# A decoder trunk on one core: order of the loads, roots and slab copies in its first stage

## The chip, the cores and the metric

The kernel runs on one core of one Trainium2 chip. The metric is the device time of one execution in microseconds. Three runs were timed, and one more execution was recorded by the hardware profiler; all readings of the trace below come from that one. The engines are named as the profile names them: PE does the matmuls (PEld loads its weights), DVE is the vector engine, ACT the scalar engine, POOL is GpSimd, and SP issues most of the DMAs.

## What is computed

One layer of a decoder over 512 positions of width 1024: a norm, one wide input projection, three groups of heads side by side (a gated delta rule, a sparse attention, a causal pooling), an output projection with a residual, a second norm and an MLP with a squared ReLU. Only the part at the start matters for this change.

```python
def rms_norm(x, g):
    xf = x.astype(jnp.float32)
    return (xf * lax.rsqrt(jnp.mean(xf * xf, axis=-1, keepdims=True) + EPS) * g).astype(x.dtype)

h = rms_norm(x, norm_mix[l])          # x: 512 x 1024
proj = h @ w_in[l]                    # w_in: 1024 x 2974, split among the heads
```

Everything is in float32.

## The kernel before

**Tiles.** The 512 positions are four tiles of 128 (`NT`), the width of 1024 is eight pieces of 128 (`KC`). A float32 product is made of three matmuls in a rounded type: each operand is split into a high part, its rounded copy, and a low part, the rest; high by high, high by low and low by high are summed.

**The first stage** (lines 153 to 330) brings x through the norm, transposes it, splits it, and multiplies it with the first slab of the projection's weights: 286 columns, loaded in two halves of 512 rows, here called slabs 0 and 1 (`dma_a`, L206). Each tile `i` goes through these steps:

- `load_x(i)` (L200): one DMA of 512 KB.
- `norm_sq(i)` (L153): the squares and their sum, on ACT (`sq`, `ss`).
- `norm_root(i)` (L159): the inverse square root of the sum. It starts from a guess made out of the bits of the number, by a shift (L164) and a multiply with add (L165) on DVE, and goes through three Newton steps of two instructions (L168 and L169 on POOL for tiles 1 to 3, L171 and L172 on DVE for tile 0).
- `norm_b(i)` (L175): x by the root and by the norm's weights `gm_b`, in two halves on DVE (`scr`, L179); then eight transposes on PE (L183).
- `norm_c(i)` (L186): the high part is copied out of PSUM by ACT (`hTh`, L191), the low part is made by DVE (`hTl`, L192).

A slab `q` is copied to its high part by ACT (`hi_a`, L210) and its low part is made by DVE (`lo_a`, L215 and L218, one instruction of 128x1144). `proj_a(i, k0, k1)` (L245) multiplies pieces `k0` to `k1` of tile `i` with them, three matmuls for each piece: 24 for a whole tile. A row of matmuls on a tile of ones (L235) stands ahead of it all.

**What sets the order.** Instructions of the first stage are recorded with `kp`, which keeps them on each engine in the order in which the program writes them; the calls from `norm_sq(0)` to `proj_a(3, 0, 8)` (L302 to L326) are that order. Each engine takes its instructions strictly in order and waits at one whose inputs aren't there. Instructions behind the first stage are placed by a scheduler, from its own estimate of when each could run; a change at the start can so move rows far behind it. The DMAs go through SP in the order written.

**What follows.** The other columns of the projection come in slabs of 256 columns (cast on ACT at L134, low part on DVE at L135, matmuls at L143 to L145), at first between the last matmuls of `proj_a`. Behind it stand the heads, up to about 385 us, and the MLP. `rsqrt` (L101), used by the heads, and `x2_norm` (L1239), used ahead of the MLP, make their first guess in the same two instructions.

Of the kernel before, what the change touches and what calls it, by code (L numbers as in the profile page):

```python
# [20 lines left out]
P = 128  # L21
# [16 lines left out]
def trunk_kernel(ctx, tc, x, norm_mix, w_in, conv_w, a_log, dt_bias, gdn_norm, nsa_q_norm, nsa_k_norm,  # L38
# [62 lines left out]
    def rsqrt(y, a, n, p=P):  # L101

        V.tensor_single_scalar(y.bitcast(I32), a.bitcast(I32), 1, ALU.logical_shift_right)
        V.tensor_scalar(y.bitcast(I32), y.bitcast(I32), -1.0, float(0x5EF759DF - 0x80000000), ALU.mult, ALU.add)
        t = sml.tile([P, n], F32, tag=f"rs{n}", name=nm("rs"))[:p]
        for _ in range(3):
            if n == 1:
                V.scalar_tensor_tensor(t, y, a, y, ALU.mult, ALU.mult)
            else:
                V.tensor_tensor(t, y, y, ALU.mult)  # L110
                V.tensor_tensor(t, t, a, ALU.mult)
            V.scalar_tensor_tensor(y, t, -1.5, y, ALU.add, ALU.mult)
# [46 lines left out]
    def norm_root(i):  # L159
# [3 lines left out]
        kp(V.tensor_scalar(ss, ss, 0.5 / D, 0.5 * EPS, ALU.mult, ALU.add))  # L163
        kp(V.tensor_single_scalar(r.bitcast(I32), ss.bitcast(I32), 1, ALU.logical_shift_right))  # L164
        kp(V.tensor_scalar(r.bitcast(I32), r.bitcast(I32), -1.0, float(0x5EF759DF - 0x80000000), ALU.mult, ALU.add))  # L165
        for _ in range(3):
# [43 lines left out]
    def hi_a(q):  # L210
        rs, hi, lo = ra[q]
        for r, k in rs:
            kp(S.copy(hi[:, k], r))

    def lo_a(q):  # L215
        rs, hi, lo = ra[q]
        for r, k in rs:
            kp(V.tensor_tensor(lo[:, k], r, f32v(hi[:, k]), ALU.subtract))  # L218
        for k in range(4):
            for c, t_ in enumerate((hi, lo)):  # L220
                slab_a[c].append(t_[:, k])

# [5 lines left out]
    S.activation(one1, one1, AF.Square)  # L228
    load_x(0)
    gm_b = bc(norm_mix[0], "gm_b", D)  # L230
    gmix = [gm_b[:, ts(b, T)] for b in range(2)]

    wps = pn()
    for _ in range(22):
        kp(PE.matmul(wps[:, 0:P], onep, onep, start=True, stop=True))  # L235
    for i in range(2):
        ra.append(dma_a(i))
        load_x(i + 1)
    load_x(3)

# [3 lines left out]

    def proj_a(i, k0, k1):  # L245

        if k0 == 0:
            aps[i] = pm()
        ps = aps[i][:, :286]
        for k in range(k0, k1):  # L250
            ah, al = hTh[:, k, ts(i, P)], hTl[:, k, ts(i, P)]
            kp(PE.matmul(ps, ah, slab_a[0][k], start=k == 0, stop=False))
            kp(PE.matmul(ps, ah, slab_a[1][k], start=False, stop=False))
            kp(PE.matmul(ps, al, slab_a[0][k], start=False, stop=k == KC - 1))

# [47 lines left out]
    norm_root(0)  # L303
    hi_a(0)
    norm_sq(1)
    norm_b(0)
    norm_root(1)
    lo_a(0)
    norm_c(0)
    hi_a(1)  # L310
    lo_a(1)
    norm_sq(2)
    norm_sq(3)
    proj_a(0, 0, 8)
    norm_b(1)
    norm_root(2)
    norm_c(1)
    proj_a(1, 0, 4)
    norm_root(3)
    norm_b(2)  # L320
    edge = norm_c(2)
    proj_a(1, 4, 8)
    edge += norm_b(3),
    proj_a(2, 0, 8)
    norm_c(3)
    proj_a(3, 0, 8)  # L326
    consts, first = ExitStack(), ExitStack()
# [911 lines left out]
    def x2_norm(i):  # L1239
# [4 lines left out]
        V.tensor_scalar(ss, ss, 0.5 / D, 0.5 * EPS, ALU.mult, ALU.add)  # L1244
        V.tensor_single_scalar(r.bitcast(I32), ss.bitcast(I32), 1, ALU.logical_shift_right)
        V.tensor_scalar(r.bitcast(I32), r.bitcast(I32), -1.0, float(0x5EF759DF - 0x80000000), ALU.mult, ALU.add)
        for _ in range(3):
# [169 lines left out]
```

## Time and profile before

| what | us |
|---|---|
| three runs | 724.2, 726.22, 729.62 |
| their median | 726.22 |
| the profiled execution | 724.06 |
| its span, from the first to the last instruction | 722.3 |
| PE busy in the span | 696.5 (96%) |
| DVE busy | 556.1 (77%) |
| ACT busy | 385.1 (53%) |
| POOL busy | 172.6 (24%) |

The busy share is an average over stages. To see what a change at the start can be worth, the stretches have to be looked at one by one, and in the first of them what each engine waits for. A row of the timeline is: start in us, length in us, engine, line and operation, what is written and read, how many; in brackets how long the engine sat idle before it, and what ended that. A row `x2` counts two instructions that follow each other. The chain of waits is followed back from the last instruction of the span: at each step to what released it, or to the instruction before it on its engine.

### The profile page before, as it was taken

What the parts mean: (1) busy time and instruction counts of PE and PEld (TensorE: products, weight loads), DVE (VectorE), ACT (ScalarE), POOL (GpSimd) and SP (SyncE); (2) the same over time, 40 slices, a digit from 0 to 9 for tenths busy, and PEclk for the clock granted to TensorE, in tenths of its full rate; (3) what the DMA queues carried; (4) which work ended last, traced back from release to release, by engine and by line L of the source; (5) the groups of instructions that cost most, each with busy time, mean ns of one, the idle gap of its engine ahead of it and who ended that gap; (6) DMA issues with size and microseconds to landing.
All of it is one profiled execution on the core that took longest, in us unless ns stands there. A gap on an engine that the chain in (4) does not pass through costs nothing.

```text
span 722.3 us, 13313 instructions
## 1 busy us (share of the span) xinstructions
PE 696.5 (96%) x5155; PEld 572.3 (79%) x5155; DVE 556.1 (77%) x1061; ACT 385.1 (53%) x768; POOL 172.6 (24%) x257
## 2 busy tenths in 40 slices
PE   8999999999999998999899999999999999999997
PEld 7888887888988776776679878888888888878885
DVE  5688998878686788887554997977958686796846
ACT  5455835565754558677543945444444444544430
POOL 5730004222123310000030330505032140504223
PEclk9999999999999999999999999999999999999999
DMA  7343223132410602221120153324041333302103
GB/s 224 91 107 103 72 60 89 32 96 60 131 31 4 234 1 59 88 88 31 59 87 2 59 176 119 114 89 144 18 158 59 120 113 113 121 23 95 58 1 116
DMA packets 49922, 62.20 MB, mean 86 GB/s; under 512 B 5494, under 2 KB 42564, under 8 KB 49860
## 3 DMA queue, kind: packets, MB, share of 16 engines
q1 hardware_dynamic: 48996, 61.16, 27.1%
q8 instruction: 40, 0.66, 0.4%
q10 hardware_dynamic: 864, 0.20, 0.1%
q14 instruction: 22, 0.18, 0.1%
HBM read 59.25 MB, written 2.10 MB: 85 GB/s over the span
## 4 chain that ended last, share of the span: by engine, by line
PE 71%; DVE 17%; DMA 4%; ACT 4%; issue 3%; POOL 1%; SPq 1%; DVEq 0%; ACTq 0%; POOLq 0%
PE ps L143 17%; PE ps L145 17%; PE ps L144 17%; PE ps L424 5%; PE ps L1139 2%; PE ps L799 2%; DMA w2r<-in_w_ffn_dram 2%; DVE bl L1293 2%; PE ps L1125 1%; DVE lw L135 1%; PE ps L587 1%; DMA x<-in_x_dram 1%; PE ps L1100 1%; ACT P L1106 1%; DVE x L1386 1%
## 5 line engine op out<-in xcount | busy, mean ns | idle before, releaser
L144 PE MATMUL ps<-h2l,hw 128*128 128x512 f32 (+1 forms) x280 | 105.1, 376 | 0.1
L145 PE MATMUL ps<-h2h,lw 128*128 128x512 f32 (+1 forms) x280 | 104.9, 376 | 0.0
L143 PE MATMUL ps<-h2h,hw 128*128 128x512 f32 (+1 forms) x280 | 103.8, 374 | 0.0
L1300 POOL TENSOR_TENSOR al<-gF,ah 128x512 fp32r<-128x512 f32 x24 | 38.1, 1586 | 220.5 <-ACT ah L1299 181.0
L143 PE MATMUL ps<-bh,ah 128*128 128x512 f32 x224 | 88.5, 395 | 1.2 <-DVE x L1386 1.2
L144 PE MATMUL ps<-bl,ah 128*128 128x512 f32 x224 | 88.2, 394 | 0.0
L145 PE MATMUL ps<-bh,al 128*128 128x512 f32 x224 | 84.6, 394 | 0.0
L1386 DVE TENSOR_TENSOR x<-ps,x 128x512 f32<-128x512 f32 x112 | 72.7, 680 | 6.0 <-PE ps L145 5.8
L1293 DVE TENSOR_TENSOR bl<-w2r,bh 128x1024 fp32r<-128x1024 f32 x40 | 57.8, 1447 | 6.1 <-ACT bh L1292 6.1
L144 PEld LDWEIGHTS ps<-h2l,hw 128*128 128x128 f32 x280 | 52.7, 188 | 10.6 <-DVE h2l L1264 0.3
L143 PEld LDWEIGHTS ps<-h2h,hw 128*128 128x128 f32 x280 | 52.3, 188 | 10.2
L145 PEld LDWEIGHTS ps<-h2h,lw 128*128 128x128 f32 x280 | 52.6, 188 | 9.7
L1300 POOL TENSOR_TENSOR al<-gS,ah 128x512 fp32r<-128x512 f32 x32 | 53.4, 1687 | 24.8 <-ACT ah L1299 23.5
L1292 ACT CAST bh<-w2r 128x1024 fp32r<-128x1024 f32 x40 | 41.8, 1047 | 24.1 <-PE ps L145 23.5
L135 DVE TENSOR_TENSOR lo<-raw,hi 128x512 fp32r<-128x512 f32 (+1 forms) x76 | 42.3, 580 | 14.4 <-ACT hi L134 11.9
L134 ACT CAST hi<-raw 128x512 fp32r<-128x512 f32 (+1 forms) x76 | 37.0, 518 | 28.5 <-DMA raw<-in_w_in_dram 10.4
L143 PEld LDWEIGHTS ps<-bh,ah 128*128 128x128 f32 x224 | 42.1, 188 | 12.1 <-ACT ah L1299 0.9
L145 PEld LDWEIGHTS ps<-bh,al 128*128 128x128 f32 x224 | 42.1, 188 | 9.7
L144 PEld LDWEIGHTS ps<-bl,ah 128*128 128x128 f32 x224 | 42.2, 188 | 9.5
L1299 ACT CAST ah<-gS 128x512 fp32r<-128x512 f32 x32 | 19.7, 620 | 50.9 <-DVE gS L1368 24.5
L134 ACT CAST hw<-raw 128x1024 fp32r<-128x1024 f32 x32 | 32.1, 1046 | 24.6 <-PE ps L144 22.2
L135 DVE TENSOR_TENSOR lw<-raw,hw 128x1024 fp32r<-128x1024 f32 x32 | 40.1, 1287 | 6.2 <-ACT hw L134 6.2
(373 smaller groups left out, 1701.9 us busy)
## 6 DMA issues: line engine op xcount, KB each, us to landing
raw<-in_w_ffn_dram SPq DMA_DIRECT2D x32, 512.0 KB, 3.8
w2r<-in_w_ffn_dram SPq DMA_DIRECT2D x32, 512.0 KB, 5.5
raw<-in_w_in_dram SPq DMA_DIRECT2D x24, 256.0 KB, 3.0
raw<-in_w_in_dram SPq DMA_DIRECT2D x36, 128.0 KB, 2.6
x<-in_x_dram SPq DMA_DIRECT2D x8, 512.0 KB, 6.7
raw<-in_cmp_w_dram SPq DMA_DIRECT2D x32, 128.0 KB, 2.7
raw<-in_w_out_dram SPq DMA_DIRECT2D x8, 512.0 KB, 4.1
out_dram<-x SPq DMA_DIRECT2D x8, 256.0 KB, 2.0
```

What stands on the lines that cost most here:

```text
L134: {"A": S.copy, "V": V.tensor_copy, "G": G.tensor_copy}[e[0]](hi[:, k], r)
L135: {"V": V, "G": G}[e[1]].tensor_tensor(lo[:, k], r, f32v(hi[:, k]), ALU.subtract)
L143: PE.matmul(ps, ah, bh, start=start, stop=False, **kw)
L144: PE.matmul(ps, ah, bl, start=False, stop=False, **kw)
L145: PE.matmul(ps, al, bh, start=False, stop=stop, **kw)
L424: PE.matmul(ps[:, ts(i, 256)], a_[:, k, ts(2 * b + i, P)], w_, start=(k == 0 and n_ == 0 and i == 0), stop=(k == KC - 1 and n_ == 2 and i ...
L799: PE.matmul(ps[halves[p], ts(s_, 64)], lhsT(halves[p], s_), rhs(halves[p], s_), start=True, stop=True)
L1292: S.copy(hi, src)
L1293: V.tensor_tensor(lo, src, f32v(hi), ALU.subtract)
L1299: S.copy(hi, src)
L1300: G.tensor_tensor(lo, src, f32v(hi), ALU.subtract)
L1386: V.tensor_tensor(x2[i][:, cs], acc[bk, t_], x2[i][:, cs], ALU.add)
```

## The change

It has five parts, all but the last in the first stage.

- The second tile of x is loaded right behind the first, ahead of `gm_b` and of the slabs.
- The first slab's high part is copied by two engines, two pieces by ACT and two by DVE. Slabs are entered in `slab_a` when they are copied, not when their low part is made.
- The order is written anew: the squares of tile 1 come ahead of the slab's copy; the scaling of tile 1 comes ahead of the low part of slab 1, as do the squares of tile 2; the root of tile 2 comes behind that low part and ahead of `norm_c(1)`. Three more matmuls on ones follow the transposes of tile 0.
- `proj_a` goes through a tile in six parts of four matmuls: three with slab 0 (high by high, high by the slab's low part, low by high), then three with slab 1, of which the last is the one that needs the low part of slab 1. For tile 0 that last part is put behind two parts of tile 1.
- The first guess of a root is one instruction: a multiply by -0.5 and an add on the bits as a number, here and in `rsqrt` and `x2_norm` (21 roots in all).

```diff
     def norm_root(i):
         kp(V.tensor_scalar(ss, ss, 0.5 / D, 0.5 * EPS, ALU.mult, ALU.add))
-        kp(V.tensor_single_scalar(r.bitcast(I32), ss.bitcast(I32), 1, ALU.logical_shift_right))
-        kp(V.tensor_scalar(r.bitcast(I32), r.bitcast(I32), -1.0, float(0x5EF759DF - 0x80000000), ALU.mult, ALU.add))
+        kp(V.tensor_scalar(r.bitcast(I32), ss.bitcast(I32), -0.5, float(0x5EF759DF - 0x80000000), ALU.mult, ALU.add))
...
     def hi_a(q):
         rs, hi, lo = ra[q]
-        for r, k in rs:
-            kp(S.copy(hi[:, k], r))
+        r = rs[0][0]
+        if q == 0:
+            kp(S.copy(hi[:, 0:2], r[:, 0:2]))
+            kp(V.tensor_copy(hi[:, 2:4], r[:, 2:4]))
+        else:
+            kp(S.copy(hi, r))
...
     load_x(0)
+    load_x(1)
     gm_b = bc(norm_mix[0], "gm_b", D)
...
-    for _ in range(22):
-        kp(PE.matmul(wps[:, 0:P], onep, onep, start=True, stop=True))
+    def warm(n):
+        for _ in range(n):
+            kp(PE.matmul(wps[:, 0:P], onep, onep, start=True, stop=True))
+
+    warm(22)
     for i in range(2):
         ra.append(dma_a(i))
-        load_x(i + 1)
-    load_x(3)
+    for i in range(2, NT):
+        load_x(i)
...
-    def proj_a(i, k0, k1):
+    def proj_a(i, n0, n1):
...
+        for n in range(n0, n1):
+            q, a_, w_ = ((0, hTh, 0), (0, hTh, 1), (0, hTl, 0), (4, hTh, 0), (4, hTl, 0), (4, hTh, 1))[n]
+            for k in range(q, q + 4):
+                kp(PE.matmul(ps, a_[:, k, ts(i, P)], slab_a[w_][k], start=(n == 0 and k == 0),
+                             stop=(n == 5 and k == KC - 1)))
...
     norm_sq(0)
     norm_root(0)
-    hi_a(0)
     norm_sq(1)
     norm_b(0)
     norm_root(1)
+    warm(3)
+    hi_a(0)
     lo_a(0)
     norm_c(0)
     hi_a(1)
+    proj_a(0, 0, 5)
+    norm_b(1)
+    norm_sq(2)
     lo_a(1)
-    norm_sq(2)
-    norm_sq(3)
-    proj_a(0, 0, 8)
-    norm_b(1)
     norm_root(2)
     norm_c(1)
-    proj_a(1, 0, 4)
+    norm_sq(3)
+    proj_a(1, 0, 2)
+    proj_a(0, 5, 6)
     norm_root(3)
+    proj_a(1, 2, 6)
     norm_b(2)
     edge = norm_c(2)
-    proj_a(1, 4, 8)
+    proj_a(2, 0, 3)
     edge += norm_b(3),
-    proj_a(2, 0, 8)
+    proj_a(2, 3, 6)
     norm_c(3)
-    proj_a(3, 0, 8)
+    proj_a(3, 0, 6)
```

Three places show what the order of the instructions becomes. The first is SP's queue at the start; before (x_92 is tile 0, x_124 tile 1; raw_121 and raw_128 are slabs 0 and 1, each in two DMAs):

```order
L202 DMA x_92<-in_x_dram 128x1024
L98 DMA gm_b<-in_norm_mix_dram 128x1024
L127 DMA raw_121<-in_w_in_dram 128x4x268
L127 DMA raw_121<-in_w_in_dram 128x4x18
L202 DMA x_124<-in_x_dram 128x1024
L127 DMA raw_128<-in_w_in_dram 128x4x268
L127 DMA raw_128<-in_w_in_dram 128x4x18
```

And now (tile 1 is x_94, slab 0 raw_123):

```order
L200 DMA x_92<-in_x_dram 128x1024
L200 DMA x_94<-in_x_dram 128x1024
L98 DMA gm_b<-in_norm_mix_dram 128x1024
L126 DMA raw_123<-in_w_in_dram 128x4x268
L126 DMA raw_123<-in_w_in_dram 128x4x18
L126 DMA raw_128<-in_w_in_dram 128x4x268
L126 DMA raw_128<-in_w_in_dram 128x4x18
```

Tile 1 went ahead of `gm_b` and of both DMAs of slab 0. The second place is DVE from the second half of tile 0's scaling to the first step of tile 2's root; before (scr_266 and scr_267 are tile 1 scaled, lo_120 and lo_127 the low parts of slabs 0 and 1, ss_235 the sum of tile 2):

```order
L179 SCALAR_TENSOR_TENSOR scr_204<-x_92,r_188,gm_b 128x512
L163 TENSOR_SCALAR ss_200<-ss_200 128x1
L164 TENSOR_SCALAR r_217<-ss_200 128x1
L165 TENSOR_SCALAR r_217<-r_217 128x1
L218 TENSOR_TENSOR lo_120<-raw_121,hi_119 128x1144
L192 TENSOR_TENSOR hTl<-ps_207,hTh 128x4x128
L192 TENSOR_TENSOR hTl<-ps_208,hTh 128x4x128
L218 TENSOR_TENSOR lo_127<-raw_128,hi_126 128x1144
L179 SCALAR_TENSOR_TENSOR scr_266<-x_124,r_217,gm_b 128x512
L179 SCALAR_TENSOR_TENSOR scr_267<-x_124,r_217,gm_b 128x512
L163 TENSOR_SCALAR ss_235<-ss_235 128x1
```

And now (scr_257 and scr_258 are tile 1 scaled, lo_122 and lo_127 the low parts, ss_271 the sum of tile 2):

```order
L177 SCALAR_TENSOR_TENSOR scr_202<-x_92,r_188,gm_b 128x512
L162 TENSOR_SCALAR ss_198<-ss_198 128x1
L163 TENSOR_SCALAR r_215<-ss_198 128x1
L213 CAST hi_121<-raw_123 128x572
L223 TENSOR_TENSOR lo_122<-raw_123,hi_121 128x1144
L190 TENSOR_TENSOR hTl<-ps_205,hTh 128x4x128
L190 TENSOR_TENSOR hTl<-ps_206,hTh 128x4x128
L177 SCALAR_TENSOR_TENSOR scr_257<-x_94,r_215,gm_b 128x512
L177 SCALAR_TENSOR_TENSOR scr_258<-x_94,r_215,gm_b 128x512
L223 TENSOR_TENSOR lo_127<-raw_128,hi_126 128x1144
L162 TENSOR_SCALAR ss_271<-ss_271 128x1
```

One instruction of the guess is gone, half a copy has come in front of slab 0's low part, and the low part of slab 1 went from before the scaling of tile 1 to behind it. The third place is PE from the transposes of tile 2 to those of tile 3; before (ps_323 and ps_324 are the transposes of tile 2, ps_353 and ps_354 those of tile 3, ps_295 the projection of tile 1, ps_363 that of tile 2; the rows left out repeat the three matmuls on ps_295 for the other pieces):

```order
L183 MATMUL ps_323<-ident,scr_319 128x128 x4
L183 MATMUL ps_324<-ident,scr_320 128x128 x4
L252 MATMUL ps_295<-hi_126,hTh 128x286
L253 MATMUL ps_295<-lo_127,hTh 128x286
L254 MATMUL ps_295<-hi_126,hTl 128x286
...
L183 MATMUL ps_353<-ident,scr_349 128x128 x4
L183 MATMUL ps_354<-ident,scr_350 128x128 x4
L252 MATMUL ps_363<-hi_119,hTh 128x286
```

And now (ps_335 and ps_336 are the transposes of tile 2, ps_366 and ps_367 those of tile 3, ps_349 is the projection of tile 2):

```order
L181 MATMUL ps_335<-ident,scr_331 128x128 x4
L181 MATMUL ps_336<-ident,scr_332 128x128 x4
L260 MATMUL ps_349<-hi_121,hTh 128x286 x4
L260 MATMUL ps_349<-lo_122,hTh 128x286 x4
L260 MATMUL ps_349<-hi_121,hTl 128x286 x4
L181 MATMUL ps_366<-ident,scr_362 128x128 x4
L181 MATMUL ps_367<-ident,scr_363 128x128 x4
L260 MATMUL ps_349<-hi_126,hTh 128x286 x4
```

Between the transposes of tiles 2 and 3 stood the second half of tile 1's projection; now it is done before them, and the first half of tile 2's stands there.

More of the change, by code (lines that the diff above doesn't have):

```diff
@@ L101, in rsqrt @@
     def rsqrt(y, a, n, p=P):
-        V.tensor_single_scalar(y.bitcast(I32), a.bitcast(I32), 1, ALU.logical_shift_right)
-        V.tensor_scalar(y.bitcast(I32), y.bitcast(I32), -1.0, float(0x5EF759DF - 0x80000000), ALU.mult, ALU.add)
+        V.tensor_scalar(y.bitcast(I32), a.bitcast(I32), -0.5, float(0x5EF759DF - 0x80000000), ALU.mult, ALU.add)
         t = sml.tile([P, n], F32, tag=f"rs{n}", name=nm("rs"))[:p]
@@ L211, in hi_a @@
         rs, hi, lo = ra[q]
-        for r, k in rs:
-            kp(S.copy(hi[:, k], r))
+        r = rs[0][0]
[4 more added lines that the diff above has]
+            kp(S.copy(hi, r))
+        for k in range(4):
+            for c, t_ in enumerate((hi, lo)):
+                slab_a[c].append(t_[:, k])
     def lo_a(q):
@@ L218, in lo_a @@
             kp(V.tensor_tensor(lo[:, k], r, f32v(hi[:, k]), ALU.subtract))
-        for k in range(4):
-            for c, t_ in enumerate((hi, lo)):
-                slab_a[c].append(t_[:, k])
     xt, xw, ra, nr, nps = {}, {}, [], {}, {}
@@ L243, in trunk_kernel @@
     aps = {}
-    def proj_a(i, k0, k1):
-        if k0 == 0:
+    def proj_a(i, n0, n1):
+        if n0 == 0:
             aps[i] = pm()
         ps = aps[i][:, :286]
[L250 to L254, printed above, removed]
+        for n in range(n0, n1):
[3 more added lines that the diff above has]
+                             stop=(n == 5 and k == KC - 1)))
     def block_mask(name, cond_pattern):
@@ L1244, in x2_norm @@
         V.tensor_scalar(ss, ss, 0.5 / D, 0.5 * EPS, ALU.mult, ALU.add)
-        V.tensor_single_scalar(r.bitcast(I32), ss.bitcast(I32), 1, ALU.logical_shift_right)
-        V.tensor_scalar(r.bitcast(I32), r.bitcast(I32), -1.0, float(0x5EF759DF - 0x80000000), ALU.mult, ALU.add)
+        V.tensor_scalar(r.bitcast(I32), ss.bitcast(I32), -0.5, float(0x5EF759DF - 0x80000000), ALU.mult, ALU.add)
         for _ in range(3):
```

## The prediction

> **What bounds the kernel now.** I read the stages first: the busy times of each engine in four stretches, cut at 25.28 us (the last tile's transposes), 120 us and 385 us. The columns are the length, then busy time and count for PE, PEld, DVE, ACT and POOL, then the granted clock.
>
> ```profile
> core 0: us, PE busy (x) PEld busy (x) DVE busy (x) ACT busy (x) POOL busy (x), PEclk, DMA share, GB/s
> 0.00:25.28 25.28, 20.43 (x116) 18.48 (x117) 14.90 (x37) 12.54 (x25) 16.08 (x65) 0.93 0.57 181
> 25.28:120.00 94.72, 94.69 (x618) 78.28 (x619) 82.44 (x193) 52.70 (x114) 20.27 (x58) 1.00 0.33 88
> 120.00:385.00 265.00, 248.90 (x2928) 203.75 (x2927) 198.82 (x556) 163.00 (x414) 45.14 (x80) 1.00 0.23 70
> 385.00:722.30 337.30, 332.47 (x1498) 271.81 (x1496) 259.95 (x276) 156.87 (x216) 91.14 (x56) 1.00 0.28 91
> ```
>
> From 25.28 to 120 us PE is busy for 94.69 of 94.72 us. Whatever lets PE enter that stretch earlier, or with less left to do, moves all behind it. From 120 to 385 us PE is idle for 265.00 - 248.90 = 16.1 us in many small waits. The change edits the first 25 us. There the chain of waits names the order of events; its columns are start, length and what.
>
> ```profile
> 2.74 6.99 DMA x<-in_x_dram
> 9.81 1.16 ACT sq L156 x2
> 11.45 0.57 DVE lo L218
> ...
> 17.29 0.21 PE ps L252
> 18.16 0.45 PE ps L183 x4
> 18.63 0.59 ACT hTh L191
> 19.25 1.29 DVE hTl L192 x2
> ...
> 24.39 0.76 DVE scr L179
> 25.28 0.64 PE ps L183 x4
> ```
>
> The second tile of x, issued fifth at 2.74 us, lands at 9.73 us; its squares, its root and then those of the next tiles follow each other down to the scaling of the fourth tile at 24.39 us (L179) and its transposes at 25.28 us. Up to there PE is fed by this chain; behind it PE is its own bound. The timeline shows how the chain runs, on DVE, then POOL (the roots of tiles 1 to 3, six small instructions each), then ACT.
>
> ```profile
> 8.09 1.42 DVE L179 SCALAR_TENSOR_TENSOR scr<-x,r,gm_b 128x512 f32<-128x512 f32 x2
> 11.45 1.35 DVE L218 TENSOR_TENSOR lo<-raw,hi 128x1144 fp32r<-128x1144 f32 x1
> 12.72 1.28 DVE L192 TENSOR_TENSOR hTl<-ps,hTh 128x512 fp32r<-128x512 f32 x2
> 13.92 1.34 DVE L218 TENSOR_TENSOR lo<-raw,hi 128x1144 fp32r<-128x1144 f32 x1
> 16.23 1.42 DVE L179 SCALAR_TENSOR_TENSOR scr<-x,r,gm_b 128x512 f32<-128x512 f32 x2 [0.97 <-POOL r L169]
> 17.74 0.15 DVE L164 TENSOR_SCALAR r<-ss 128x1 int32<-128x1 int32 x1
> 17.93 0.15 DVE L165 TENSOR_SCALAR r<-r 128x1 int32<-128x1 int32 x1
> 20.90 1.42 DVE L179 SCALAR_TENSOR_TENSOR scr<-x,r,gm_b 128x512 f32<-128x512 f32 x2
> ```
>
> ```profile
> 11.63 1.39 POOL L168 TENSOR_SCALAR rs<-r,ss 128x1 f32<-128x1 f32 x1 [3.77 <-DVE r L165]
> 13.92 1.47 POOL L169 TENSOR_SCALAR r<-rs,r 128x1 f32<-128x1 f32 x1
> 15.93 0.27 POOL L169 TENSOR_SCALAR r<-rs,r 128x1 f32<-128x1 f32 x1
> 18.18 0.34 POOL L168 TENSOR_SCALAR rs<-r,ss 128x1 f32<-128x1 f32 x1 [1.99 <-DVE r L165]
> 20.24 0.26 POOL L169 TENSOR_SCALAR r<-rs,r 128x1 f32<-128x1 f32 x1
> 21.08 1.29 POOL L168 TENSOR_SCALAR rs<-r,ss 128x1 f32<-128x1 f32 x1 [0.58 <-DVE r L165]
> ```
>
> A POOL step of one element takes 0.27 or 0.34 us, but 1.3 to 1.5 us when DVE subtracts a slab (11.45, 13.92) or scales a tile (20.90): POOL stands still until DVE is through. Beside hTl at 12.72, which reads PSUM, it doesn't. An undisturbed root is that of tile 2: first step at 18.18, last ending at 20.50, so 2.32 us, of which 1.98 after the first step.
>
> **The change, part by part.** *Loads.* The transfers reach about 340 GB/s once they run; the row gives the GB/s in 40 bins of 1.125 us from the start.
>
> ```profile
> GB/s 0 55 215 379 329 322 346 381 343 347 404 293 69 49 17 34 298 151 15 0 0 15 15 28 1 25 287 155 0 51 233 186 62 0 15 7 32 224 234 199
> 4.71 1.06 ACT L156 ACTIVATE sq<-x 128x1024 f32<-128x1024 f32 x1 [2.42 <-DMA x<-in_x_dram]
> 8.53 1.15 ACT L213 CAST hi<-raw 128x1144 fp32r<-128x1144 f32 x1 [2.66 <-DMA raw<-in_w_in_dram]
> ```
>
> A tile of x is 512 KB, 1.5 us at that rate. The first tile was there at 4.71; second in the queue, tile 1 should land near 6.2 us, not 9.73. The norm weights gm_b and the first slab stand one tile later each: the slab at 8.5 + 1.5 = 10.0. When gm_b landed is not shown, only that it was by 8.09; by the same rate it was there at 6.2, so 7.7 now. It may be as late as 8.09 + 1.5 = 9.6. I take 7.7, which leaves the root of tile 0 in front.
>
> *One-step first guess.* Of each root one DVE instruction goes, 0.15 us long, 0.19 from start to start (17.74 to 17.93). Tile 0's root ends 0.19 earlier, and its scaling runs from 7.9 us, with some slack 8.1 to 9.5.
>
> *Root of tile 1.* Its squares are done by 7.7 us, so its two DVE steps follow the scaling at once, to 9.9 us, and POOL could begin at 10.0 where it began at 11.63. But at 10.0 the slab lands, and DVE turns to it: its half of the copy, 572 elements, a form that the trace doesn't have. Its bounds are 0.37 us (the f16 copies below, 0.249 us for 384) and 0.67 (half of the 1.35 for 1144 with two operands); I take 0.5, nearer to a copy. ACT's half is 1.15/2 = 0.6. Then the subtraction runs from 10.65 to 12.0 and hTl of tile 0 to 13.3.
>
> ```profile
> L810 DVE COPY W<-id x14: 240/249/469, 35.4 to 38.4; 128x384 f16<-128x384 f16 x14
> L103 DVE TENSOR_SCALAR r<-ss x11: 136/170/311, 136.0 to 279.9; 128x8 int32<-128x8 int32 x4, 128x6 int32<-128x6 int32 x4, 128x4 int32<-128x4 int32 x2, 64x1 int32<-64x1 int32 x1
> ```
>
> POOL's first step ends at 12.0 as in the row at 11.63, the other five 1.98 us later, at 14.0, and tile 1 is scaled from 14.05 instead of 16.23: 2.2 us earlier. The second slab's subtraction is now behind that scaling and holds POOL no more (the row at 13.92 cost this root 1.2 us).
>
> Here a rule speaks against the change. The Trainium skill (GPSIMD Engine Reference, Specifications) says that GpSimd shares its SBUF interfaces with VectorE and contends with DVE instructions of two SBUF inputs or in a two-port mode, and its page VectorE: DVE Perf Modes (Mode 2×_2P) puts an fp32 copy within SBUF in that mode. By the first the copy on DVE would hold POOL too, and by the second it would take about 0.30 us, an estimate from the page's two elements a cycle at 0.96 GHz; the time would be 721.9, 0.2 below the sum at most, from the shorter copy. The rows at 11.63 and 13.92 agree on the two inputs; none here shows a two-port copy beside POOL.
>
> *Roots of tiles 2 and 3.* The second slab's subtraction (1.34) runs from 15.5 to 16.85, the two steps of tile 2's root to 17.2, POOL to 17.3 + 2.32 = 19.6, and tile 2 is scaled from 19.65, not 20.90: 1.25 us earlier. The third root starts on POOL beside that scaling and is held until 21.1 as in the row at 21.08, then takes 1.98: 23.1. Tile 3 is scaled from 23.15, not 24.39, and its transposes start 1.2 us earlier.
>
> *PE's order.* The projection now goes by halves and parts, so that only the fifth part of tile 0 waits for the second slab's low part. Ahead of the last transposes PE now does 24 + 24 + 12 matmuls instead of 24 + 24 (front, the PE rows). A warm one costs:
>
> ```profile
> 28.02 0.29 PE L252 MATMUL ps<-hi,hTh 128*128 128x286 f32 x1
> 29.60 0.30 PE L252 MATMUL ps<-hi,hTh 128*128 128x286 f32 x1
> ```
>
> twelve steps in 1.58 us, 0.132 each. So 12 x 0.132 = 1.6 us of work leaves the stretch in which PE is the bound. These twelve need hTl of tile 2 (20.4 + transposes, ACT, DVE: by 23.1), still before the transposes at 24.05.
>
> *The three extra warm matmuls* are six records of 8.01/44 = 0.18 us, 1.1 us.
>
> ```profile
> 1.12 8.01 PE L235 MATMUL ps<-onep 128*128 128x128 f32 x44 [1.12 <-DVE one L227]
> 11.49 0.40 PE L252 MATMUL ps<-hi,hTh 128*128 128x286 f32 x1 [1.27 <-ACT hTh L191]
> 10.54:13.95 3.41, 1.29 (x5) 0.87 (x6) 2.88 (x7) 3.40 (x7) 2.02 (x4) 0.99 0.85 311
> 13.95:17.37 3.42, 3.42 (x17) 3.42 (x16) 2.45 (x4) 1.33 (x4) 2.04 (x3) 0.51 0.16 39
> ```
>
> They lie where PE waits for hTh (1.27 us idle before 11.49) and cost nothing; without that cover they would push tile 0's first product by 1.1 us, which still ends before hTl at 13.3. The last two rows show why they are there: 3.41 us with PE busy for 1.29, then 3.42 us at a granted clock of 0.51. In that cold stretch the matmuls of tile 0 held the transposes of tile 1 back until 18.0 (18.16 in the chain), although its first half was scaled by 16.95 (16.23 and half of 1.42).
>
> *Roots elsewhere* lose 0.17 us each (row L103), 17 of them. Before 120 us PE hides them. Behind, a few stand ahead of PE; I take 0.3 us, between 0 and 17 x 0.17 = 2.9.
>
> **The sum** is 1.2 + 1.6 + 0.3 = 3.1 us. The profiled execution took 724.06 us (its span is 722.3, 1.8 lie around it), so 721.0 by its own clock. It is the lowest of the four times shown (724.06, 724.2, 726.22, 729.62); the median of the three runs is 2.2 above it and that of all four is 725.2, 1.15 above. A forecast of a median is best set against the latter: 725.2 - 3.1 = 722.1 us.
>
> **Rivals.** (a) *The slabs don't follow.* PE gets 1.6 us ahead of the chain that also starts the slabs' casts; if it then waits for them, only 1.2 + 0.3 stays: 723.7. For it speaks that DVE is busy for 82.44 of 94.72 us there; against it that PE waits for 0.03 us in that stretch now. (b) *The new order behind 120 us waits more*, and this one ends slower. The scheduler places everything after the start anew, and PE takes its work strictly in order. PE idles 16.1 us there now; a third more is 5.4, net 725.2 - 3.1 + 5.4 = 727.5. It decides from 19.2 us of idle on. Nothing in the profile of before tells which way it goes. (c) The same the other way: a fifth less idle, 3.2 us, gives 718.9. (d) *The clock gate.* If the cold stretch moves under the last 36 matmuls of the projection, a matmul takes between 0.20 us (17 records in 3.42) and 0.26 (0.132 at 0.51 of the clock); at 0.24 it costs 36 x 0.11 = 4 us: 726.1. The row at 10.54 went cold after 1.29 of 3.41 us; in the new order the emptiest such stretch, 20.7 to 24.1, holds 1.3 us of transposes and 1.6 of matmuls, 85%, so against it. The Trainium skill (TensorE: Matmul & The Clock Gate, What's actually happening, and Part 4: PE-mode transpose) says that the window is free-running, 3413 ns, and that transposes don't count as busy; by that only 1.6 of 3.4 would count, nearer to the cold row. (e) *gm_b is late* at 9.6: tile 0 is scaled to 11.0, the two steps, the copy, the subtraction and hTl go to 14.5, and POOL, held until 13.2, ends the root at 15.2. Tile 1 is scaled 1.2 later, tile 3 with it: 723.3, inside the forecast's own range.
>
> **How the numbers follow.** Forecast with (e), 720 to 724: 0.52. (a) 0.15, (b) 0.12, (c) 0.13, (d) 0.08. The time is that of the first, 722.1. The range leaves out the far ends of (b) and (c): 717.5 to 727.5. One per cent of 726.22, 7.3 us, is about what a measurement of this kernel can tell from no change. Faster than 718.9 takes (c) at its full price: 0.11. Slower than 733.5 takes twice the price of (b): 0.04. Within 1%: 0.85.
>
> **What would show it.** Right: squares of tile 1 ahead of the first slab's copy, near 6.3 us; tile 1 scaled near 14, tile 2 near 19.7, tile 3 near 23.2; PE still without idle to 120 us; a clock of 1.00 after 14 us. Wrong: PE waiting between the last transposes and 120 us (a), a scaling of tile 0 after 9 us (e), a row at half clock after 20 us (d), or an idle of PE from 120 to 385 us that differs from 16 by more than 3 (b, c).

## The result and the profile after

| kernel | median of the runs, us | lowest to highest | profiled execution | its span |
|---|---|---|---|---|
| before | 725.29 (6 runs) | 723.56 to 729.62 | 724.06 | 722.3 |
| after | 720.59 (6 runs) | 720.12 to 720.69 | 720.69 | 718.7 |

The ratio is 0.9938, with a 95% interval of 0.9921 to 0.9955: 0.6% less, some 4.7 us, so within the 1% that was counted as no change. The forecast was 722.1 in a range of 717.5 to 727.5. By the two profiled executions the gain is 724.06 - 720.69 = 3.4 us (3.6 in the spans), against 3.1 in the sum.

The stages of after, cut at the same times as before's; the columns are the length, then busy time and count for PE, PEld, DVE, ACT and POOL, the granted clock, the DMA share and GB/s.

```profile
0.00:25.28 25.28, 22.42 (x150) 20.17 (x151) 16.34 (x38) 13.55 (x28) 16.88 (x75) 1.00 0.57 183
25.28:120.00 94.72, 93.64 (x664) 75.74 (x663) 83.30 (x193) 56.47 (x124) 22.82 (x53) 1.00 0.34 88
120.00:385.00 265.00, 249.63 (x2878) 205.30 (x2878) 198.91 (x544) 158.74 (x406) 40.81 (x74) 0.99 0.22 70
385.00:718.70 333.70, 329.33 (x1475) 268.87 (x1473) 256.02 (x268) 156.20 (x212) 89.66 (x56) 1.00 0.28 92
```

In the first stretch PE is busy for 2.0 us more than before and the clock is 1.00 instead of 0.93: the stretch at half clock at 14 us is gone. (Another one stands in the third stretch, from 209.79 to 213.21 us, where before has none.) In the second PE now idles for 94.72 - 93.64 = 1.08 us, where it idled for 0.03. In the third it idles for 15.4 us (16.1 before).

The chain of waits of after, over the first 24 us (start, length, what):

```profile
2.66 7.22 DMA raw<-in_w_in_dram
...
9.96 0.68 ACT hi L212
...
10.65 1.39 DVE lo L223
...
12.09 2.48 PE ps L260 x16
14.57 0.45 PE ps L181 x4
...
15.04 0.59 ACT hTh L189
...
15.68 4.00 PE ps L260 x28
19.68 0.64 PE ps L181 x4
...
22.24 0.75 DVE scr L177
22.99 0.14 issue
23.13 0.64 PE ps L181 x4
```

Its head is no longer tile 1 of x but the first slab's load, landing at 9.88 us. Tile 1's root is not on it, and between 12 and 20 us PE itself is: its matmuls run nearly without a pause. The last transposes start at 23.13 us, 2.15 before their old place. The timeline of DVE shows what each scaling waited for (in brackets the idle time and what ended it):

```profile
8.02 1.41 DVE L177 SCALAR_TENSOR_TENSOR scr<-x,r,gm_b 128x512 f32<-128x512 f32 x2 [0.43 <-DMA gm_b<-in_norm_mix_dram]
9.97 0.47 DVE L213 CAST hi<-raw 128x572 fp32r<-128x572 f32 x1 [0.29 <-DMA raw<-in_w_in_dram]
10.65 1.38 DVE L223 TENSOR_TENSOR lo<-raw,hi 128x1144 fp32r<-128x1144 f32 x1 [0.22 <-ACT hi L212]
13.39 1.41 DVE L177 SCALAR_TENSOR_TENSOR scr<-x,r,gm_b 128x512 f32<-128x512 f32 x2 [0.16 <-POOL r L167]
18.79 1.41 DVE L177 SCALAR_TENSOR_TENSOR scr<-x,r,gm_b 128x512 f32<-128x512 f32 x2 [1.03 <-POOL r L167]
20.96 1.36 DVE L190 TENSOR_TENSOR hTl<-ps,hTh 128x512 fp32r<-128x512 f32 x2 [0.77 <-ACT hTh L189]
22.24 1.41 DVE L177 SCALAR_TENSOR_TENSOR scr<-x,r,gm_b 128x512 f32<-128x512 f32 x2
```

And the timeline of POOL, from the root of tile 1 (9.78) to that of tile 3 (18.72):

```profile
9.78 0.34 POOL L166 TENSOR_SCALAR rs<-r,ss 128x1 f32<-128x1 f32 x1 [1.89 <-DVE r L163]
10.23 0.33 POOL L167 TENSOR_SCALAR r<-rs,r 128x1 f32<-128x1 f32 x1
10.66 1.51 POOL L166 TENSOR_SCALAR rs<-r,ss 128x1 f32<-128x1 f32 x1
...
13.09 0.27 POOL L167 TENSOR_SCALAR r<-rs,r 128x1 f32<-128x1 f32 x1
...
18.72 0.86 POOL L166 TENSOR_SCALAR rs<-r,ss 128x1 f32<-128x1 f32 x1
19.69 0.64 POOL L167 TENSOR_SCALAR r<-rs,r 128x1 f32<-128x1 f32 x1
...
21.69 0.27 POOL L167 TENSOR_SCALAR r<-rs,r 128x1 f32<-128x1 f32 x1
```

The root of tile 1 got two of its six steps done before the subtraction at 10.65 held the third until 12.17, so it ended at 13.36. The root of tile 3 began 0.07 us before the scaling that was to hold it, and ended at 21.96; the scaling that uses it started at 22.24, when DVE was through with hTl of tile 2 (20.96 to 22.32).

**Where the 3.6 us of the span went.** Two landmarks cut both traces at the same work: the last transposes, and the first squares of the second norm (`x2_norm`, at the end of the heads). Their rows in after, of PE's and ACT's timelines:

```profile
23.13 1.29 PE L181 MATMUL ps<-ident,scr 128*128 128x128 f32 x8 [0.28 <-DVE scr L177]
```

```profile
360.83 1.06 ACT L1253 ACTIVATE sq<-x 128x1024 f32<-128x1024 f32 x1 [3.31 <-DVE x L1224]
```

In before, those squares start at 363.53 us. So 2.15 us came up to the transposes, 338.25 - 337.70 = 0.55 between the landmarks and 358.77 - 357.87 = 0.9 behind them. In the middle part PE idles for 15.00 us instead of 14.62 and is busy for 322.70 us instead of 323.63. So of the 1.6 us of matmuls that left this part only 0.93 us shows as less busy time. After has its stretch at half clock here, before has its own ahead of the transposes; that the rest went into it fits, but is not shown.

### The profile page after: what moved, and what is told of

It is laid out like the page before. It is cut to its first block, busy times and chain, and to the rows that moved or that the text cites. A ratio compares the mean times of both kernels' runs of the same rounds, so it can differ in the third digit from the quotient of the medians.

```text
span 718.7 us, 13300 instructions
## 1 busy us (share of the span) xinstructions
PE 695.0 (97%) x5161; PEld 570.1 (79%) x5161; DVE 554.6 (77%) x1041; ACT 385.0 (54%) x768; POOL 170.2 (24%) x257
## 4 chain that ended last, share of the span: by engine, by line
PE 80%; DVE 10%; ACT 3%; DMA 3%; issue 2%; POOL 0%; SPq 0%; DVEq 0%; ACTq 0%; POOLq 0%
PE ps L142 19%; PE ps L143 18%; PE ps L144 18%; PE ps L434 7%; PE ps L809 3%; PE ps L1149 2%; PE ps L260 2%; PE ps L597 1%; PE ps L1135 1%; DMA raw<-in_w_in_dram 1%; ACT P L1116 1%; DMA raw<-in_cmp_w_dram 1%; DVE lw L134 1%; DVE bl L1302 1%; PE ps L1110 1%
## 5 line engine op out<-in xcount | busy, mean ns | idle before, releaser
L1309 POOL TENSOR_TENSOR al<-gF,ah 128x512 fp32r<-128x512 f32 x24 | 36.4, 1516 | 224.0 <-ACT ah L1308 184.6
L134 DVE TENSOR_TENSOR lo<-raw,hi 128x512 fp32r<-128x512 f32 (+1 forms) x76 | 43.0, 587 | 11.0 <-ACT hi L133 10.4
L134 DVE TENSOR_TENSOR lw<-raw,hw 128x1024 fp32r<-128x1024 f32 x32 | 41.2, 1321 | 5.8 <-ACT hw L133 5.7
```

The source lines that it names most:

```text
L134: {"V": V, "G": G}[e[1]].tensor_tensor(lo[:, k], r, f32v(hi[:, k]), ALU.subtract)
L1309: G.tensor_tensor(lo, src, f32v(hi), ALU.subtract)
```

## The experiments

Twelve kernels were run. Each was timed beside before on the same chip. The last transposes and the squares of the second norm are the two landmarks, read from the profiled execution. That is one execution of several, and in u_split, u_order and b_warm the longest of them; f_ab's is the second longest of twelve.

| kernel | median, us | before beside it | ratio [95%] | last transposes start | from there to the squares | profiled execution, us | its mean clock |
|---|---|---|---|---|---|---|---|
| before | 725.29 | | | 25.28 | 338.25 | 724.06 | 0.998 |
| after | 720.59 | 725.29 | 0.9938 [0.9921, 0.9955] | 23.13 | 337.70 | 720.69 | 0.997 |
| u_load | 723.79 | 724.97 | 0.9987 [0.9970, 1.0005] | 24.82 | 339.86 | 724.28 | 0.992 |
| u_guess | 724.56 | 724.97 | 0.9998 [0.9977, 1.0020] | 24.07 | 339.99 | 724.15 | 0.999 |
| u_split | 725.12 | 724.97 | 1.0009 [0.9989, 1.0028] | 23.77 | 344.96 | 728.78 | 0.984 |
| u_fill | 736.92 | 724.97 | 1.0156 [1.0125, 1.0187] | 23.64 | 354.10 | 737.38 | 0.985 |
| u_order | 734.08 | 724.62 | 1.0114 [1.0076, 1.0151] | 23.67 | 355.05 | 738.65 | 0.978 |
| u_warm | 721.34 | 724.62 | 0.9954 [0.9937, 0.9971] | 22.95 | 337.28 | 720.00 | 1.000 |
| m_gmb | 720.37 | 724.62 | 0.9936 [0.9914, 0.9957] | 23.12 | 337.18 | 720.09 | 0.998 |
| b_warm | 736.09 | 724.62 | 1.0157 [1.0122, 1.0192] | 26.54 | 351.91 | 738.70 | 0.979 |
| f_ba | 726.14 | 725.25 | 1.0010 [0.9995, 1.0024] | 25.19 | 339.84 | 726.14 | 0.993 |
| f_ab | 722.26 | 725.25 | 0.9973 [0.9957, 0.9989] | 22.97 | 342.87 | 725.81 | 0.990 |
| f_fill | 723.62 | 725.25 | 0.9977 [0.9964, 0.9990] | 23.61 | 340.28 | 723.82 | 0.994 |
| f_order | 721.89 | 725.25 | 0.9954 [0.9937, 0.9972] | 24.12 | 338.77 | 723.14 | 0.995 |

Kernels with the same first stage differ there by up to 0.5 us from one trace to another (u_order and f_order), since the loads land earlier or later: the copy of the first slab starts at 9.69 us in u_order, 9.96 in after, 10.09 in f_order and 10.51 in u_fill. Counted from that copy the spread is gone: the last transposes start 13.17 us behind it in after, 13.1 to 13.2 in u_warm, m_gmb, f_ab, u_fill and f_fill, 13.4 in u_split, 13.8 in u_guess and 14.0 in u_order and f_order.

### One part undone, the rest placed by the scheduler

**u_load**: after, with tile 1 of x fifth in the queue again.

```diff
     load_x(0)
-    load_x(1)
     gm_b = bc(norm_mix[0], "gm_b", D)
...
-    for i in range(2, NT):
-        load_x(i)
+        load_x(i + 1)
+    load_x(3)
```

> The changed kernel with the second tile of x loaded fifth again, all else kept. Chain theory: its squares wait for the landing near 9.7 us and stand ahead of the slab's copy on ACT, so the slab is copied from 11.0, tile 1 is scaled near 14.6 us instead of 13.4, the last transposes start near 24.3 instead of 23.1, and the time is 1.2 us more than the changed kernel's 720.6: 721.8. Rival, that the gain comes from the order behind 120 us and the start matters little: the start moves by 1.2 us too, but the time moves by what PE's idle time from 120 to 385 us moves, in either direction.

Measured: 723.79, so 3.2 us above after. The last transposes start 1.7 us later, where 1.2 was expected. So much the early load is worth at the start; the 1.5 us that are left over lie behind it, in an order that changed too, and can't be put down to the load.

**u_guess**: after, with the first guess of all 21 roots in two instructions again.

```diff
-        V.tensor_scalar(y.bitcast(I32), a.bitcast(I32), -0.5, float(0x5EF759DF - 0x80000000), ALU.mult, ALU.add)
+        V.tensor_single_scalar(y.bitcast(I32), a.bitcast(I32), 1, ALU.logical_shift_right)
+        V.tensor_scalar(y.bitcast(I32), y.bitcast(I32), -1.0, float(0x5EF759DF - 0x80000000), ALU.mult, ALU.add)
```

> The changed kernel with the first guess of all 21 roots in two instructions again. Chain theory: tile 0's scaling waits for gm_b anyway and tile 3's for DVE, so the roots of tiles 1 and 2 move by 0.2 us each and the last transposes by 0.2 to 0.4 us; with the other roots 0.3 more: 721.2, between 720.8 and 723.5. Rival (the instructions removed from the roots elsewhere are what gained): over 723.

Measured: 724.56, 4.0 us above after and outside what was expected. Of this 0.9 lies ahead of the last transposes (0.6 counted from the slab's copy), where the sum had 0.19 for one root. But 17 roots of 0.17 us can't give 3 us unless each stood ahead of PE, and the order behind the first stage changed with them. f_ab below has the two instructions behind the first stage only, in another order, and took 722.26. So what the guess alone is worth was not separated.

**u_split**: after, with the first slab's high part copied by ACT alone.

```diff
-            kp(S.copy(hi[:, 0:2], r[:, 0:2]))
-            kp(V.tensor_copy(hi[:, 2:4], r[:, 2:4]))
+            kp(S.copy(hi, r))
```

> The changed kernel with the first slab's high part copied by ACT alone. Chain theory: the copy takes 1.15 us instead of 0.67, the low part starts 0.5 us later, tile 1 is scaled near 13.8 instead of 13.4, the last transposes start 0.4 us later: 721.0. Rival (the copy's half on DVE holds POOL's root back, so the split gains nothing): tile 1 is scaled at 13.4 or earlier, 720.6 or less.

Measured: 725.12, 4.5 above after, with the last transposes only 0.6 later (0.2 counted from the copy). In the profiled execution, the longest of ten, the rest is lost between the landmarks, at a mean clock of 0.984. A copy that ends half a microsecond later can't cost 4.5 us where it stands; what the split itself is worth was not separated.

**u_fill**: after, with the first half of tile 2's projection behind the last transposes instead of ahead of them.

```diff
-    proj_a(2, 0, 3)
     edge += norm_b(3),
-    proj_a(2, 3, 6)
+    proj_a(2, 0, 6)
```

> The changed kernel with the first half of tile 2's projection behind the last transposes again. Chain theory: the twelve matmuls, 1.6 us, fall back into the stretch in which PE is the bound, while the last transposes start at 23.0: 722.1. Rival (the slabs can't follow, so PE waits there for them instead): 720.6, with PE's idle time moved from ahead of the transposes to behind them.

Measured: 736.92, 16.3 us above after. The edit moves twelve matmuls, 1.6 us of work. The table shows where the rest is: 354.10 us from the transposes to the squares, 16.4 more than in after.

**u_order**: after, with the low part of slab 1 ahead of tile 1's scaling.

```diff
     proj_a(0, 0, 5)
+    lo_a(1)
     norm_b(1)
     norm_sq(2)
-    lo_a(1)
```

> The changed kernel with the low part of slab 1 ahead of the scaling of tile 1 on DVE again, all else kept. Chain theory: tile 1 is scaled near 14.6 us instead of 13.4, but the two steps of tile 2's root still come at 16.0, since DVE has the same work to do before them; tile 2 is scaled at 18.8 as now and the last transposes start within 0.3 us of 23.1: 720.6 to 720.9. Rival (the scaling of tile 1 sets the end of the start): the last transposes 1.2 us later, 721.8.

Measured: 734.08, 13.5 above after. Up to the last transposes it lost 0.5 us, or 0.8 counted from the slab's copy. It too lost the rest between the landmarks.

**u_warm**: after, without the three extra warm matmuls (no other row moves).

```diff
     norm_root(1)
-    warm(3)
     hi_a(0)
```

> The changed kernel without the three matmuls on ones behind tile 0's transposes; no other instruction changes its place. Chain theory: they cost nothing and PE has enough to do without them, so nothing changes: 720.6 with a clock of 1.00 after 10 us. Clock rival: a stretch of 3.4 us at half clock follows near 14 us, the projection of tiles 0 and 1 runs at half pace, the last transposes start 0.5 to 1.5 us later: 721.1 to 722.1.

Measured: 721.34, but its ten runs go from 720.0 to 723.11, and the intervals of u_warm and after overlap. The clock stayed at 1.00 in the first 25 us without them, as with them. They neither cost nor save what could be told.

**m_gmb**: after, with `gm_b` ahead of tile 1 in SP's queue.

```diff
-    load_x(1)
     gm_b = bc(norm_mix[0], "gm_b", D)
+    load_x(1)
```

> The changed kernel with gm_b loaded ahead of the second tile of x; SP's queue alone changes. Chain theory: tile 0 is scaled at 7.6 instead of 8.0 us, but the chain starts at the slab's landing near 9.9, which stays: the last transposes start at 23.1 within 0.1, 720.6. Rival (the scaling of tile 0 is on the chain): 0.4 us earlier, 720.2.

Measured: 720.37, the same. Tile 0 was scaled at 7.78 instead of 8.02, and tile 1 at 13.40 instead of 13.39: the later landing of `gm_b` cost nothing.

**b_warm**: before, with three warm matmuls behind the transposes of tile 0.

```diff
+    for _ in range(3):
+        kp(PE.matmul(wps[:, 0:P], onep, onep, start=True, stop=True))
```

> The kernel before with three more matmuls on ones behind the transposes of tile 0. Theory that the half clock from 13.95 to 17.37 us costs the kernel before its time: the projection of tile 0 ends 1.0 to 1.5 us earlier, the transposes of tile 1 start near 17.0 instead of 18.0, the last transposes 0.3 to 1.0 us earlier, and the runs spread less: about 724.6 against 725.3. Rival (the stretch is off the chain, or comes whatever PE does): the clock is half there again or the last transposes start at 25.3 as before; 725.3.

Measured: 736.09, 11.5 above before. They don't keep the clock up in the old order; it goes to half at 12.67 us instead of 13.91, and for twice as long. Windows of b_warm around it (columns as above):

```profile
9.26:12.67 3.41, 1.57 (x11) 1.17 (x10) 1.47 (x4) 3.26 (x6) 0.90 (x1) 1.00 1.11 367
12.67:16.08 3.41, 3.08 (x11) 2.77 (x12) 2.73 (x4) 1.66 (x4) 2.91 (x6) 0.50 0.35 108
16.08:19.49 3.41, 3.41 (x17) 3.40 (x16) 1.78 (x5) 1.08 (x2) 1.20 (x4) 0.50 0.42 129
```

That costs 1.3 us by the last transposes. The other 10 or more are between the landmarks again.

### The same starts, with the order behind them held

In four of these kernels a small edit cost 4 to 16 us far behind its place, and no expectation had that. Either the start was worth that much in a way that the traces don't show, or the scheduler, which places everything behind the first stage anew, had made another order that is worse by itself. To tell these apart, four kernels have a table that fixes the order of every instruction behind the first stage, on each engine, to that of before or that of after. This adds ordering between neighbours of one engine, and no instruction. Neither before nor after was run with its own order fixed in this way, so what the fixing itself may cost is not shown. In all four the number of instructions of a first guess behind the first stage goes with that order (one in after's, two in before's).

**f_ba**: the first stage of before, and behind it the order of after. **f_ab**: the first stage of after, and behind it the order of before.

```diff
+    mark = len(nc.cur_bb.bb.instructions)
...
+    for part in zlib.decompress(base64.b85decode(ORDER)).decode().split(";"):
+        e_, steps = part.split(":")
+        at_, prev = -1, None
+        for d_ in steps.split(","):
+            at_ += int(d_)
+            if prev is not None:
+                tc.add_manual_dep(rows[e_][at_], prev.name,
+                                  mybir.DependencyInfo(mybir.DependencyClass.NoSync, mybir.DependencyReason.DATA),
+                                  reason="order")
+            prev = rows[e_][at_]
```

> The first stage of the kernel before (loads, two-step guess of the four first roots, slab copy by ACT alone, old order, no extra warm matmuls), and behind it all instructions in exactly the order that the changed kernel has on each engine, with its one-step guesses there. Start theory (the start is worth the 2.2 us by which the last transposes move and the 1.6 us of PE work done before them, if the order behind is the same): 720.6 + 3.7 = 724.3, last transposes at 25.3. Order theory (what the change gains or loses is decided by the order behind): 720.6 within 1. The chain theory of the runs before (start and order both good): between.

> The changed first stage, and behind it all instructions in exactly the order of the kernel before, with its two-step guesses there. Start theory: 724.7 - 3.7 = 721.0, last transposes at 23.1 us, PE without idle to 120 us but for what the slabs can't follow. Order theory: 724.7 within 1.

Measured: 726.14 and 722.26. With before and after this is a table of two by two.

| | order behind as in before | order behind as in after |
|---|---|---|
| first stage of before | 725.25 | 726.14 |
| first stage of after | 722.26 | 720.59 |

The new start alone, in the old order, is worth 3.0 us by the medians and 2.0 by the ratio of 0.9973 (its interval, 0.9957 to 0.9989, makes it 0.8 to 3.1). The two differ because f_ab's runs fall in two groups: eight of 721.2 to 723.2 at a mean clock of 0.997 to 1.000, and four of 724.3 to 726.0 at 0.990 to 0.994. The new order alone is worth nothing that can be told (0.9995 to 1.0024). In the new order the start is worth 726.14 - 720.59 = 5.5. So the gain comes from the start. Both kernels came out slower than the theory of the start had it (724.3 for f_ba, 721.0 for f_ab), by 1.8 and 1.3 us. The two parts don't simply add: the new order takes 1.7 us off with the new start, which its intervals barely tell from nothing (0.9957 is f_ab's lower end, 0.9955 after's upper one), and adds 0.9 with the old. Why is not shown as a whole; one piece is in the waits below.

The waits of PE from 25.28 to 120 us in f_ba (us in total, times, the longest) settle another point:

```profile
PE ps L706 <- PE ps L188: 0.8, 1, 0.8
PE ps L227 <- DVE scr L223: 0.6, 1, 0.6
PE ps L778 <- POOL qd L823: 0.3, 1, 0.3
```

And those of after:

```profile
PE ps L671 <- PE ps L143: 0.8, 1, 0.8
PE ps L743 <- POOL qd L788: 0.3, 1, 0.3
```

The lines of f_ba are shifted by 35 or 45; the first and third waits are after's two. (The second is the old late transposes.) They are there with the old start too, so they belong to the new order, and aren't what PE pays for being early. The trace names PE itself as the releaser of the longer one, so what held it isn't shown.

In the old order the new start does make PE wait. These are the waits of f_ab in the same stretch, where before waits only for the old late transposes:

```profile
PE ps L856 <- ACT T L889: 1.0, 1, 1.0
PE ps L188 <- ACT hi L179: 0.6, 1, 0.6
```

The second is a wait for a slab's high part (L179 is after's L134), at 44.97 us: PE had come there before the cast. So rival (a) is real in the old order, at 0.6 us. The first, with the smaller waits behind it, stands ahead of two windows at half clock, 121.84 to 128.67 us, in this execution.

**f_fill** and **f_order**: the starts of u_fill and u_order (the same edits), with the order of after behind them.

```diff
-    proj_a(2, 0, 3)
     edge += norm_b(3),
-    proj_a(2, 3, 6)
+    proj_a(2, 0, 6)
```

> The changed kernel with the first half of tile 2's projection behind the last transposes, as in u_fill, and behind the first stage the order of the changed kernel on each engine. Start theory: 1.6 us of work and the 0.5 us by which the last transposes came later there: 722.2 to 722.7; the rest of the 16 us that u_fill lost was the order that the scheduler gave it. Rival (the moved matmuls themselves cost it): near 736.

```diff
+    lo_a(1)
     norm_b(1)
     norm_sq(2)
-    lo_a(1)
```

> The changed kernel with the low part of slab 1 ahead of the scaling of tile 1, as in u_order, and behind the first stage the order of the changed kernel on each engine. Start theory: 0.3 to 0.5 us, as its last transposes moved: 720.9 to 721.1; the rest of what u_order lost was its order. Rival (the moved instruction itself costs it): near 734.

Measured: 723.62 where u_fill took 736.92, and 721.89 where u_order took 734.08, with the same start to within 0.5 us. So 13 of u_fill's 16 us and 12 of u_order's 13.5 are the order that the scheduler made behind the start. What is left is what the edits are worth at their place, with whatever the fixing costs: 3.0 us above after for f_fill (the intervals don't meet), and 1.3 for f_order (they overlap).

f_fill's 3.0 is more than the 1.6 us of its matmuls, and windows of its trace show why:

```profile
20.50:24.00 3.50, 1.31 (x11) 0.89 (x9) 2.73 (x5) 2.12 (x9) 2.79 (x18) 1.00 0.07 17
24.00:27.50 3.50, 3.50 (x18) 3.26 (x16) 2.99 (x7) 2.11 (x4) 2.92 (x10) 0.51 0.09 14
27.50:31.00 3.50, 3.50 (x29) 3.50 (x28) 0.01 (x1) 1.46 (x5) 2.76 (x13) 1.00 0.47 145
```

With nothing to do ahead of the last transposes PE is busy for 1.31 of 3.50 us, and is then granted half the clock while it is fully loaded, which costs up to 1.7 us more. The Trainium skill (TensorE: Matmul & The Clock Gate, What's actually happening) describes a free-running window of 3413 ns after which the clock is set; the stretch at 0.51 here is about that long.

**What the bad orders lose.** The stage of the heads in u_order:

```profile
120.00:385.00 265.00, 244.37 (x2786) 198.86 (x2784) 188.78 (x508) 153.86 (x384) 40.63 (x68) 0.94 0.20 64
```

and in f_order:

```profile
120.00:385.00 265.00, 249.69 (x2867) 205.04 (x2867) 197.91 (x540) 158.97 (x407) 40.76 (x74) 0.99 0.22 70
```

PE idles for 20.6 us instead of 15.3, which is 5.3 more, and the clock is 0.94 instead of 0.99. Over the whole span the mean clocks give (1 - 0.978) x 736.7 = 16.2 us of withheld clock against (1 - 0.995) x 721.2 = 3.6, 12.6 more. The two add up to 17.9, and the profiled executions differ by 15.5; some of the half clock falls on idle time. So in this execution the greater part of the loss is not the waiting, but the half clock behind it. It is the longest of u_order's four, though. The other three, of 731.3 to 734.3 us, had mean clocks of 0.991 to 0.993. On average they took 11.2 us more than the four of f_order, with 3.4 us more of withheld clock, so in them most of the loss is not the clock. One of the places in u_order, in windows of 3.41 us:

```profile
284.56:287.97 3.41, 1.83 (x13) 1.14 (x11) 2.48 (x10) 3.38 (x10) 0.00 (x0) 1.00 0.00 0
287.97:291.38 3.41, 2.92 (x11) 2.26 (x12) 3.41 (x12) 3.41 (x12) 0.00 (x0) 0.50 0.11 11
291.38:294.79 3.41, 3.41 (x11) 2.40 (x10) 3.35 (x10) 2.84 (x6) 0.00 (x0) 0.50 0.76 234
```

The waits that stand at that place, 280 to 325 us:

```profile
PE ps L936 <- DVE sm L1089: 1.8, 1, 1.8
PE ps L142 <- ACT yTh L147: 1.5, 1, 1.5
PE ps L1135 <- DVE r L111: 1.4, 1, 1.4
```

f_order has a granted clock of 1.00 there.

## Why the prediction was right, point by point

**The landings.** Right: the first slab's copy starts at 9.96 us (10.0 was worked out), the squares of tile 1 at 5.88 (6.3), the scaling of tile 0 at 8.02, waiting for `gm_b` (7.9, with some slack). Rival (e), `gm_b` at 9.6, didn't come about, and m_gmb shows that its place costs nothing.

**DVE's half of the copy.** Right in size: 0.47 us, where 0.5 was taken between 0.37 and 0.67. The rule against it was right about the hold and short on the time. By the Trainium skill's two elements a cycle (VectorE: DVE Perf Modes, Mode 2×_2P) 0.30 was the estimate; with the 0.15 us that an instruction of one element takes on DVE it comes to 0.45, close to the row. The hold on POOL, from the Trainium skill's GPSIMD Engine Reference (Specifications), is there: the POOL step beside the copy ends 0.12 to 0.13 us after the copy does, whenever it began, in after, m_gmb, f_ab and u_order alike. In after it began late, at 10.23, and took 0.33 us instead of 0.27. In m_gmb, with the same first stage but for `gm_b`, it began at 10.10 and took 0.48:

```profile
10.10 0.48 POOL L167 TENSOR_SCALAR r<-rs,r 128x1 f32<-128x1 f32 x1
10.00 0.46 DVE L213 CAST hi<-raw 128x572 fp32r<-128x572 f32 x1 [0.44 <-DMA raw<-in_w_in_dram]
```

So the hold cost the root 0.06 us in after and 0.2 in m_gmb, and no more, since the copy is short. The subtraction behind it held the next step for 1.51, as the page and the rows of before have it.

**The scalings.** Each was earlier than forecast: 13.39, 18.79 and 22.24 against 14.05, 19.65 and 23.15. One step of the working made most of this. "POOL's first step ends at 12.0 as in the row at 11.63" took the whole root as held; two of six steps were through before the subtraction came, which made tile 1 0.66 us earlier, and tiles 2 and 3 follow it. The other step, "the third root starts on POOL beside that scaling and is held until 21.1", failed by little: the root's first step came 0.07 us ahead of the scaling, was held (0.86 us) only until the first half of the scaling was through, and the second step went beside the other half (0.64 us). The root ended 1.1 us earlier than forecast, of which 0.86 is the earlier scaling of tile 2. The rest gained nothing: what stands ahead of tile 3's scaling is now DVE itself, with hTl of tile 2 until 22.32.

**The term of 1.2 us** for the earlier transposes was thus mis-sized: it measured 2.15.

**The term of 1.6 us** for twelve matmuls filled in ahead of the transposes was of the right kind, and f_fill confirms it: undone alone, it costs 3.0 us, with a window at half clock among them which the term didn't have. How much of the 3.0 is the matmuls alone wasn't separated.

**The term of 0.3 us** for the roots elsewhere can't be read from any run: the 0.9 us behind the second landmark hold it and the spread.

**PE without idle to 120 us.** Wrong: 1.08 us. This looked like rival (a), in which the slabs don't follow, but f_ba has the same two waits with the old start; they come with the new order. Rival (a) shows only in f_ab, with 0.6 us for one slab.

**The clock.** Right at the start: 1.00 throughout the first 25 us, and the window ahead of the last transposes held; the twelve matmuls are in it. But a row at half clock after 20 us, which was named as a sign of (d), did come, at 209.79 us, in the heads and not under the projection that (d) was about. f_fill shows rival (d) at work where the twelve matmuls are taken out.

**The order behind 120 us.** The idle of PE changed by 0.7 us (16.1 to 15.4), so neither (b) nor (c) came about. But the case was under-priced: "a third more is 5.4" counted the waits alone. The orders of u_fill and u_order cost 13 and 12 us by themselves, and b_warm's some 10 by its landmarks; part of u_order's went through the half clock that follows a wait, which that price left out (12.6 us more of it withheld than in f_order by the profiled executions, 3.4 by the others). Three of the seven orders that the scheduler made in these runs (u_load, u_guess, u_split, u_fill, u_order, b_warm, after) were so bad, where 0.12 was the chance given to (b). The forecast came out right with an order that is as good as the old one, and nothing in the profile of before could tell that it would be: this part was luck.

**The sum.** 1.2 + 1.6 + 0.3 = 3.1 against 4.7 in all. Without the roots elsewhere it is 2.8, against 2.0 to 3.0 for the new start in the old order and 5.5 in the new one. So the mechanism holds: the start gains, by earlier transposes and by matmuls done ahead of them. That the number came close is in part luck: the term for the transposes was too small by 0.95 us, waits of PE that the sum didn't have took some back, and the clock, which it left out, moved too. By (1 - mean clock) x span the 28 executions of before beside f_ab have 4.4 us of withheld clock on average, the six of after 1.8. How much of the 4.7 us is this difference of 2.6 is not shown.

## What to carry to other kernels

Where a scheduler places what follows, an edit at the start is two edits: its own few microseconds, and a new order behind, which here cost up to 13 us; fix the order behind before the size of a small edit is measured or believed. Price a wait on PE with what it does to the clock: waits that add up to some 2 us can cost 1.7 us again when the half clock behind them meets a fully loaded PE. Steps of one engine that another engine's long instruction holds should be followed one by one: those that come before it are through, as two of six were here. And one profiled execution can be the longest of its kernel; look at the mean clocks of the others before a cause is read from it.

## What the runs showed that was not expected

The half clock came behind windows in which PE had been busy for 1.31 of 3.50 us (f_fill), 1.57 of 3.41 (b_warm) and 1.83 of 3.41 (u_order), none of them an idle window: the longest single wait in these was 2.15 us. Not each such window brings it: m_gmb has one of 1.83 us, 203.54 to 206.95, with a clock of 1.00 behind it. In b_warm the half clock then lasted for two windows; PE was busy for 3.08 us of the first.

The stretches keep to a beat of 3.41 us. Those of u_order begin at 175.33, 209.47, 287.97, 308.45, 335.76 and 366.48 us; the distances between them are whole multiples of 3.413 us to within 0.02, and each stretch lasts for one or two of them. Whether a wait falls into one window or is shared by two so differs from one execution to the next, which may be why runs of one kernel differ; that was not tested.

After has one such stretch too, in the heads, whose order is new; in before the clock is 1.00 there. The windows of after around it:

```profile
206.38:209.79 3.41, 1.30 (x42) 0.96 (x42) 3.34 (x13) 0.19 (x1) 0.00 (x0) 1.00 0.00 0
209.79:213.21 3.42, 3.42 (x52) 3.30 (x51) 2.31 (x8) 1.71 (x5) 1.74 (x4) 0.50 0.00 0
```

PE waits there for 1.3 us for one tile of DVE's, and for 0.8 for another. Whether filling it would gain the 1.7 us that the half clock takes was not tried.
